# Weight sums moved from GpSimd to VectorE, kept in DRAM and reloaded; forms reloaded in place; one activation table for Ln and Exp

## The chip, the cores and the metric

One core of a Trainium2 chip runs the kernel. The metric is the device time in microseconds (us) of one execution. A core's engines work in parallel, each on its own queue of instructions in a fixed order: TensorE (PE, with its weight loads as PEld), VectorE (DVE), ScalarE (ACT), GpSimd (POOL) and SyncE (SP), which here issues all DMAs.

## The reference

One layer of a diffusion trunk, in float32, over 2048 latent tokens and 256 context tokens of 1024 channels:

```python
h = rmsnorm(x, norm_g) * (1 + scale) + shift          # hc likewise from ctx
v, g_b, g_c, z_a, u, z_b, m_a, m_b = split(h @ w_in)  # eight blocks of 1024
xc = grid_conv(u, conv4_w, 2) + conv4_b
y_lru = forward and backward RG-LRU scans of xc, started from the context's final states
y_a = g_b * grid_conv(g_c * v, conv3_w, 1) * silu(z_a)
y_b = y_lru * silu(z_b)
merged = sigmoid(m_a) * (y_a @ w_out_a) + sigmoid(m_b) * (y_b @ w_out_b)
x = rmsnorm(x + gate * (merged @ w_o), final_g)
```

shift, scale and gate come from a product of silu(c) with w_ada. An RG-LRU direction has two block-diagonal gates (128x128 blocks), a decay a = exp(-8 r softplus(-lambda)) and a linear recurrence over the tokens.

## The kernel before, in words

**Arithmetic.** Channels lie on the 128 partitions (8 blocks of channels, K = 8, H = 4), tokens along the free axis in four tiles of 512 (T), two tiles to a half. Each float32 matrix is split into a rounded part and a rest (`split2`, L426: ACT copies x to hi as fp32r, DVE subtracts lo = x - hi), and a product is three passes: hi hi, lo hi, hi lo (`passes`, L462).

**Pairs.** In the sweeps and in the second projection a product of two blocks of output channels with two token tiles is made with seven half products in place of eight (`class Pair`, L531; p1 to p7, each 12 matmuls of 512 columns). For that the tokens are combined into seven *forms* (B11, B21, B22, T1 to T4, four tiles each, with hi and lo 56 tiles), and the weights of two output blocks, r1 and r2, into parts A to D. Part A is r1 itself. `prep_d` (L547) makes the sums: s = r2's upper plus lower half (this is D), r2's upper half from r1 minus r2 (r2 is then C), and two more that turn r1 into B: four additions of 128x512 in a chain, all on POOL (`TT(..., eng="POOL")`, L274). `prep_a`, `prep_d`, `prep_bc` then split A, D, B, C.

**Order.** `sweep(half, c)` (L1030) treats channel block c of one half of the tokens with four pairs: L (LRU input and merge gate A), G (conv C gate and value), B (conv B gate and SiLU gate), Z (LRU SiLU gate and merge gate B). Between the pairs stand the gates' matmuls (bdp), convolutions, decays and scans. Eight first sweeps (half 0; block 0 starts with plain products, and only its Z is a pair) are followed by the projection of y_a (`merged_a`, L1181), eight second sweeps (half 1), `merged_a(1)`, `merged_b(1)` (L1192, four pairs ob10 to ob13), the output product `wo1`, `merged_b(0)` (pairs ob00 to ob03) and the last output product with the final norms (L1369 to L1408). In the first sweeps the context's 256 tokens of the same block run too: `ctx_gemm` (L708) multiplies raw r1 of the L pair, in float32, with the modulated context, four tiles hc that are kept in hc_dram and reloaded for each block from 1 on; three conv steps, gates and scans follow.

**Forms in DRAM.** T3, T4 and B22 go through fm_dram: `rest` (L1021) loads each into a T tile and then splits it with `put` into two F tiles. `gathered` (L1136) does the same with ya and with half of mg.

**Memory.** Tiles come from pools of numbered slots (SLOTS, L31): T 17 tiles of 128x512, F 64 of the same size in fp32r, W 6 of 128x1024 (split weights), D 2 of 128x512 (split D), R 3 of 128x1024 (raw weights), S 1 of 128x512 (s). A pool's buffers take their slots in the order in which the program first writes them.

**Planner.** Nothing is issued as written: every operation goes to `Plan` (L81) with an engine and a cost (`act_us`, `dve_us`, POOL 0.2 + 0.0027 a column, a DMA by its KB). `once` (L142) is a list scheduler: PE keeps the order of the program, and on ACT, DVE, POOL and SP the operation that can start first goes first, ties by how late it may be. A DMA that needs a slot is held back to 18 us ahead of PE (AHEAD). What it finds is each engine's fixed order on the chip, where an instruction waits for its semaphores, and all behind it on that engine too. TABLE (L36) gives Ln and Exp different tables, and a switch costs 1.3 in the plan.

**Norms.** `Stats` (L500) sums squares (ACT squares, DVE or, for x2, x3 and the context, POOL adds); `rs` sums over partitions with a product by ones (tile ss), and `rsq` (L480) makes the inverse root by Ln, Exp(-0.5 .) and three DVE steps.

Of the kernel before, what the change touches and what calls it, by code (L numbers as in the profile page):

```python
# [8 lines left out]
F32 = mybir.dt.float32  # L9
# [6 lines left out]
P = 128  # L16
D = 1024
# [18 lines left out]
TABLE = {AF.Sigmoid: "sigmoid", AF.Exp: "exp", AF.Tanh: "exp", AF.Sqrt: "sqrt", AF.Ln: "ln"}  # L36


class Buf:
# [214 lines left out]
def trunk(ctx: ExitStack, tc: tile.TileContext, par, sel2, xT, ctxT, wada, wgate, crow, win, woa, wob, wo, lru, out):  # L254
# [109 lines left out]
    pk_dram = dram("pk_dram", K, 2, 3, P, T)  # L364
    yb_dram = dram("yb_dram", 2, K, 2, P, T)
    mg_dram = dram("mg_dram", 2, K, 2, P, T)
    pa_dram = dram("pa_dram", 2, K, 2, P, T)
    z_dram = dram("z_dram", K, 2, P, T)
    kept = {}
# [60 lines left out]
    def put(name, x, bias=None):  # L430
# [6 lines left out]
            STT(lo.v, x, bias, hi.v, AD, SU)  # L437
        return hi, lo

    def fetch(name, src, kb=512, after=()):  # L440
        r = Buf("R", name)
        DMA(r.v, src, kb, after)
        return r

# [84 lines left out]


    class Pair:  # L531
        def __init__(self, name, s1, s2, after=()):
            self.name, self.s1, self.s2 = name, s1, s2
            self.r1 = fetch(name + "r1", s1, after=after)
            self.r2 = None
            self.after = after

        def second(self):
            if self.r2 is None:
                self.r2 = fetch(self.name + "r2", self.s2, after=self.after)  # L540

        def prep_a(self):
            n = self.name
            self.fa = Buf("W", n + "Ah"), Buf("W", n + "Al")
            split2(self.fa[0].v, self.fa[1].v, self.r1.v, 2 * T)

        def prep_d(self):  # L547
            n = self.name
            self.second()
            r1, r2 = self.r1, self.r2  # L550
            s = self.s = Buf("S", n + "s1")
            TT(s.v, r2[:, :H, :], r2[:, H:, :], AD, eng="POOL")
            TT(r2[:, :H, :], r1[:, :H, :], r2[:, :H, :], SU, eng="POOL")
            TT(r1[:, :H, :], s.v, r1[:, :H, :], SU, eng="POOL")
            TT(r1[:, H:, :], r1[:, H:, :], r1[:, :H, :], SU, eng="POOL")
            self.fd = Buf("D", n + "Dh"), Buf("D", n + "Dl")
            split2(self.fd[0].v, self.fd[1].v, s.v)

        def prep_bc(self):
            n = self.name  # L560
            self.fb = Buf("W", n + "Bh"), Buf("W", n + "Bl")
# [63 lines left out]
    class Lru:  # L625
# [79 lines left out]
            return i  # L705


        def ctx_gemm(self, raw, hcs=None):  # L708
# [10 lines left out]
            self.split("c", xc[:, :CTX], CTX)  # L719

        def ctx_gates(self, d):
            c = self.c
# [122 lines left out]
        return r  # L845

    def raw0(name, src):
        r = Buf("R", "r" + name)
        queue(DMA(r.v, src, 512))
        return r  # L850

    def matvec(m):

        row = ps(f"row{m}")
        for k0 in (0, H):
            mms = [(sc[:, k, :], wc[m, k].v, k0 == 0, k0 == H) for k in range(k0, k0 + H)]
            ins = [sc.v] + [x for _, x, _, _ in mms] + ([row.v] if k0 else [])

            def emit(mms=mms):
                for j, (w, x, a, z) in enumerate(mms):  # L860
# [3 lines left out]
        rows = Buf("S", f"rows{m}")  # L864
        rv = rows.m(lambda t: t.rearrange("p a b -> p (a b)"))
        A(rv, row.v, AF.Copy)
        return rv
# [147 lines left out]
        DMA(dbuf("fm_dram", 0, j), x21, 256)  # L1015
    raw = fetch("rawL", win[4 * K])
    lr.ctx_gemm(raw, hcs)
    a = unit("aZA1", wZA, bt1)
    cv.za(1, a.v)

    def rest(form, kinds, biased=True):  # L1021

        for n, i in kinds:
            for j in range(H):
                x = tb(n + "x")
                DMA(x.v, dbuf("fm_dram", i, j), 256)
                form[n].append(put(f"{n}_{j}", x.v, shf(H + j) if i == 2 and biased else None))


    def sweep(half, c, state, form):  # L1030

        plain_start = half == 0 and c == 0
        ss = srcs(c)
        n = f"{half}{c}"
        lr, cv = state["lr"], state["cv"]
        tail = state.pop("tail", [])
        pl = pg = None
        if plain_start:
            rest(form, (("T3", 1), ("T4", 0)))
            pz = Pair("Z" + n, *ss[3])  # L1040
            pz.p1(form)
            lr.ctx_gates(0)
        else:
            pl = state.pop("pl", None) or Pair("L" + n, *ss[0])
# [16 lines left out]
            pg = Pair("G" + n, *ss[1])  # L1061
# [11 lines left out]
            pb = Pair("B" + n, *ss[2])  # L1073
# [12 lines left out]
            lr.decay(1)  # L1086
            za1 = pb.p7(form)
            pz = Pair("Z" + n, *ss[3])
            pz.p1(form)
            cv.za(0, pb.p4(form).v)  # L1090
            lr.forward(1)
# [26 lines left out]
                lr.forward(1)  # L1118
            state["tail"][0] = late
        if c + 1 < K:  # L1120
            nl = state["lr"] = Lru(half, c + 1)
            state["cv"] = Conv(half, c + 1)
            nl.weights()
            if half == 0:
                state["pl"] = Pair(f"L{half}{c + 1}", *srcs(c + 1)[0])
                nl.ctx_gemm(state["pl"].r1)

    def stats(t):
        s = Stats(f"x{t}", eng="POOL")
# [4 lines left out]
        return s  # L1134

    def gathered(key, half, k, t, name):  # L1136
        x = tb(name)
        DMA(x.v, dbuf(key, half, k, t), 256)
        return put(name, x.v)
# [326 lines left out]
```

## Time and profile before

| | |
|---|---|
| runs, median (range) | 1947.99 us (1946.63 to 1950.41), 3 runs |
| profiled execution, own time | 1946.85 us |
| its span | 1945.1 us |
| PE busy | 1895.3 us, 97% |
| DVE busy | 1579.1 us, 81% |
| ACT busy | 1135.8 us, 58% |
| POOL busy | 507.3 us, 26% |
| DMA | 307.89 MB, 158 GB/s over the span |

The span runs from the first to the last instruction of the profiled execution; its own time is the device time of that execution. Busy times are unions of instructions on an engine; matmuls overlap each other, and their ends are modelled. L277 is the line of `TT`, so all additions of tiles stand under it, on POOL or DVE; L284 is `STT`, L271 ACT's `A`, L319 PE's `MM`, L327 the DMAs. Tiles carry the pair's name: G05r is the raw weight of pair G of half 0, block 5, Ah and Al its split part A, y, x, z its PSUM tiles, a and u what is copied out of them.

### The profile page before, as it was taken

The numbers are of one execution on the slowest core, as the hardware profiler recorded it, in microseconds if no ns is written. First come the engines' busy times: TensorE is split into PE (matmuls) and PEld (weight loads), VectorE is DVE, ScalarE is ACT, GpSimd is POOL, SyncE is SP. The second block draws the span as 40 slices with busy tenths as digits, with TensorE's granted clock in tenths as the row PEclk, the third lists the DMA queues.
The fourth block names the chain that finished last, engine by engine and source line by source line (L and its number), as shares of the span: only waits on it lengthen the run. The fifth ranks groups of instructions, "written<-read, shape, count | busy, mean of one in ns | idle before, by whom it ended". The sixth has DMA issues, their size and how long they took to land.

```text
span 1945.1 us, 24314 instructions
## 1 busy us (share of the span) xinstructions
PE 1895.3 (97%) x8546; PEld 1558.2 (80%) x8546; DVE 1579.1 (81%) x2050; ACT 1135.8 (58%) x1604; POOL 507.3 (26%) x305
## 2 busy tenths in 40 slices
PE   6999999999999999999999999999999999999997
PEld 3777888888888888888888888888888888788787
DVE  6897877878687878868898988989898778769854
ACT  6589676767677777346556575565756333435332
POOL 0222332332524230023233333242341022012100
PEclk9999999999999999999999999999999999999998
DMA  9152414233342416851442514324243985777933
GB/s 346 60 197 87 136 65 141 87 131 116 122 155 84 136 65 232 298 194 48 154 146 76 169 54 157 123 100 150 73 157 118 345 307 184 258 249 243 337 115 117
DMA packets 145419, 307.89 MB, mean 158 GB/s; under 512 B 16272, under 2 KB 20496, under 8 KB 145296
## 3 DMA queue, kind: packets, MB, share of 16 engines
q1 hardware_dynamic: 145296, 306.34, 45.9%
q8 instruction: 67, 1.10, 0.2%
q14 instruction: 56, 0.46, 0.1%
HBM read 218.19 MB, written 88.08 MB: 157 GB/s over the span
## 4 chain that ended last, share of the span: by engine, by line
PE 69%; DVE 13%; DMA 8%; ACT 6%; issue 4%; SPq 0%; POOL 0%; DVEq 0%; ACTq 0%; POOLq 0%
PE oa L319 9%; PE ao L319 4%; PE bdp L319 4%; PE wo L319 3%; ACT L271 2%; DVE xc L284 2%; DVE i L303 1%; DMA wc<-wada 1%; PE ac L319 1%; DMA pal<-pa_dram 1%; DMA pk<-pk_dram 1%; DMA x<-xT 1%; DMA mg<-mg_dram 1%; DMA sb<-smb_dram 1%; PE Z17y L319 1%
## 5 line engine op out<-in xcount | busy, mean ns | idle before, releaser
L271 ACT ACT_TABLE_LOAD x152 | 195.0, 1283 | 3.6 <-PEq L1457 0.7
L303 DVE TENSOR_TENSOR_SCAN i<-a,st,i 128x512 f32<-128x512 f32 x48 | 77.3, 1623 | 0.0
L277 DVE TENSOR_TENSOR i<-i,r 128x512 f32<-128x512 f32 x64 | 67.7, 1059 | 0.0
L284 DVE SCALAR_TENSOR_TENSOR r<-a,r 128x512 f32<-128x512 f32 x64 | 47.0, 755 | 16.9 <-ACT r L271 16.9
L271 ACT ACTIVATE xh<-xc 128x512 fp32r<-128x512 f32 x32 | 20.2, 632 | 58.0 <-DVE xc L284 58.0
L277 DVE TENSOR_TENSOR i<-i,xc 128x512 f32<-128x512 f32 x64 | 51.4, 822 | 0.4 <-ACT i L271 0.4
L271 ACT ACTIVATE a<-r,ns 128x512 f32<-128x512 f32 x64 | 46.0, 720 | 0.7 <-DVE i L277 0.2
L271 ACT ACTIVATE r<-bdp,pr 128x512 f32<-128x512 f32 x64 | 44.0, 687 | 1.3
L271 ACT ACTIVATE i<-bdp,pr 128x512 f32<-128x512 f32 x64 | 44.0, 687 | 0.0
L271 ACT ACTIVATE r<-r,hs 128x512 f32<-128x512 f32 x64 | 43.2, 712 | 0.0
L284 DVE SCALAR_TENSOR_TENSOR zz<-ao,gates,xr 128x256 f32<-128x256 f32 (+1 forms) x24 | 13.7, 572 | 35.1 <-PE ao L319 34.5
L271 ACT ACTIVATE sq<-zz 128x256 f32<-128x256 f32 (+1 forms) x21 | 10.3, 488 | 50.0 <-DVE zz L284 49.9
L271 ACT ACTIVATE r<-r 128x512 f32<-128x512 f32 x64 | 37.7, 624 | 0.4
L277 DVE TENSOR_TENSOR xl<-xc,xh 128x512 fp32r<-128x512 f32 x32 | 32.1, 1002 | 3.7 <-ACT xh L271 3.7
L277 DVE TENSOR_TENSOR sa<-oa,sa 128x512 f32<-128x512 f32 x32 | 21.7, 685 | 13.2 <-DMA sa<-sma_dram 7.0
L277 DVE TENSOR_TENSOR y<-y,sg 128x512 f32<-128x512 f32 x32 | 29.0, 907 | 0.0
L284 DVE SCALAR_TENSOR_TENSOR ri<-acc,ri 128x256 f32<-128x256 f32 x16 | 7.1, 452 | 26.3 <-ACT ri L271 26.3
L277 DVE TENSOR_TENSOR yx<-yx,yx 128x512 f32<-128x512 f32 x32 | 24.2, 758 | 4.5 <-DMA yx<-yb_dram 2.3
L277 POOL TENSOR_TENSOR ob00s<-ob00r 128x512 f32<-128x512 f32 x1 | 1.3, 1304 | 92.5 <-DMA fm_dram<-yx 92.5
L277 POOL TENSOR_TENSOR ob10s<-ob10r 128x512 f32<-128x512 f32 x1 | 1.3, 1287 | 88.4 <-DMA ob10r<-wob 88.4
L277 POOL TENSOR_TENSOR L10s<-L10r 128x512 f32<-128x512 f32 x1 | 1.3, 1294 | 87.5 <-DMA L10r<-win 87.5
L303 DVE TENSOR_TENSOR_SCAN pk<-pk,st,pk 128x512 f32<-128x512 f32 x16 | 20.4, 1277 | 4.5 <-DMA pk<-pk_dram 4.5
(15371 smaller groups left out, 7400.4 us busy)
## 6 DMA issues: line engine op xcount, KB each, us to landing
pk<-pk_dram SPq DMA_DIRECT2D x48, 256.0 KB, 5.6
wc<-wada SPq DMA_DIRECT2D x32, 256.0 KB, 6.0
ya_dram<-y SPq DMA_DIRECT2D x32, 256.0 KB, 3.3
pk_dram<-i SPq DMA_DIRECT2D x32, 256.0 KB, 2.2
roa<-woa SPq DMA_DIRECT2D x16, 512.0 KB, 4.5
ya<-ya_dram SPq DMA_DIRECT2D x32, 256.0 KB, 5.1
sa<-sma_dram SPq DMA_DIRECT2D x32, 256.0 KB, 5.0
pa_dram<-sa SPq DMA_DIRECT2D x32, 256.0 KB, 5.2
```

The source lines that it names most:

```text
L271: act.activation(o.ap(), i.ap(), func, **kw)
L277: return plan.add(Op(eng, d, lambda: e.tensor_tensor(o.ap(), a.ap(), b.ap(), op=op)), [o], [a, b])
L284: dve.scalar_tensor_tensor(o.ap(), a.ap(), s.ap() if isinstance(s, V) else s, b.ap(), op0=op0, op1=op1, **kw)
L303: dve.tensor_tensor_scan(o.ap(), a.ap(), u.ap(), init.ap() if isinstance(init, V) else init, op0=M, op1=AD)
L319: pe.matmul(o.ap(), w.ap(), x.ap(), start=a, stop=z, skip_group_check=True)
```

## The change

- **Sums on DVE.** `TT` sends every addition to DVE, whatever eng says: the four sums of each pair, the squares of x2, x3 and the context, and the four T1 differences of block 0.
- **Sums kept.** A pair of the first sweeps gets `at=(i, c)` and stores s, r1 (now B) and r2 (now C) to wd_dram, wb_dram and wc_dram after the sums: 28 pairs of blocks 1 to 7 and Z of block 0. The same 29 pairs of the second sweeps are made with `old=True`: they load A from the input and D, B, C from DRAM, each into a slot of the pool of its parts, and make no sums. L, G and B of block 0 in half 1, and the eight pairs of the projections, still make their sums (on DVE), without storing them.
- **Pools.** R and S are gone; W has 9 slots and D 3. Raw weights now take slots of W, s one of D, in one order with the split parts.
- **Forms in place.** `put_from` loads a form, ya or mg into the F tile that becomes its lo part, and splits there. No T tile is used.
- **Context of block 1.** Its L weight is fetched, and its `ctx_gemm` run, right behind that of block 0, with the context's tiles still on chip; the split follows later, where the product stood before.
- **One table.** In `rsq`, Ln and Exp are given the same table in the plan, and that set, natural_log_exp_and_others, is loaded by name ahead of the first of them.

```diff
-SLOTS = {"T": (17, (P, T), F32), "F": (64, (P, T), F32R), "W": (6, (P, K, P), F32R), "D": (2, (P, H, P), F32R),
-         "R": (3, (P, K, P), F32), "S": (1, (P, H, P), F32), "ps": (6, (P, T), F32), "bd": (2, (P, T), F32)}
+SLOTS = {"T": (17, (P, T), F32), "F": (64, (P, T), F32R), "W": (9, (P, K, P), F32R), "D": (3, (P, H, P), F32R),
+         "ps": (6, (P, T), F32), "bd": (2, (P, T), F32)}
...
     def TT(o, a, b, op, n=T, eng="DVE"):
-        e = {"DVE": dve, "POOL": pool}[eng]
+        eng = "DVE"; e = dve
...
+    def put_from(name, src, bias=None):
+        lo, hi = fb(name + "l"), fb(name + "h")
+        raw = lo.m(lambda t: t.bitcast(F32))
+        DMA(raw, src, 256)
+        if bias is None:
+            split2(hi.v, lo.v, raw)
+        else:
+            A(hi.v, raw, AF.Identity, bias=bias)
+            STT(lo.v, raw, bias, hi.v, AD, SU)
+        return hi, lo
...
     def rsq(r, ss, tmp, n=T):
-        A(r, ss, AF.Ln, bias=epsd.v, scale=1.0 / D, n=n)
-        A(r, r, AF.Exp, scale=-0.5, n=n)
+        for op in (A(r, ss, AF.Ln, bias=epsd.v, scale=1.0 / D, n=n), A(r, r, AF.Exp, scale=-0.5, n=n)):
+            op.table = LN_EXP
...
         def prep_d(self):
             n = self.name
-            self.second()
+            if self.old:
+                rd, self.rb, self.rc = (self.land(p, f, dbuf(f"w{f.lower()}_dram", *self.at), kb)
+                                             for p, f, kb in (("D", "D", 256), ("W", "B", 512), ("W", "C", 512)))
+                self.fd = self.part("D", "D", rd, T)
+                return
+            self.r2 = fetch(n + "r2", self.s2, after=self.after)
...
+            if self.at:
+                for t, r, kb in (("wd_dram", s, 256), ("wb_dram", r1, 512), ("wc_dram", r2, 512)):
+                    DMA(dbuf(t, *self.at), r.v, kb)
...
     lr.ctx_gemm(raw, hcs)
+    pl1, lr1 = Pair("L01", *srcs(1)[0], at=(0, 1)), Lru(0, 1)
+    lr1.ctx_gemm(pl1.r1, hcs, False)
...
-                x = tb(n + "x")
-                DMA(x.v, dbuf("fm_dram", i, j), 256)
-                form[n].append(put(f"{n}_{j}", x.v, shf(H + j) if i == 2 and biased else None))
+                form[n].append(put_from(f"{n}_{j}", dbuf("fm_dram", i, j), shf(H + j) if i == 2 and biased else None))
...
+        def pair(i, c=c):
+            return Pair("LGBZ"[i] + f"{half}{c}", *srcs(c)[i], at=(i, c) if c or i == 3 else None,
+                        old=half == 1 and (c > 0 or i == 3))
...
+    loaded = None
     for op in order:
+        if op.table and op.table != loaded:
+            loaded = op.table
+            if loaded == LN_EXP:
+                act.preload_act_table_set(LN_EXP)
```

## Rows read from the trace of the kernel before

**Rows 1.** The page, busy time of each engine, share of the span and instructions:
```profile
PE 1895.3 (97%) x8546; PEld 1558.2 (80%) x8546; DVE 1579.1 (81%) x2050; ACT 1135.8 (58%) x1604; POOL 507.3 (26%) x305
```

**Rows 2.** Windows by stage: length, busy PE, PEld, DVE, ACT, POOL, PEclk, DMA, GB/s:
```profile
60.00:180.00 120.00, 113.64 (x504) 92.43 (x503) 105.50 (x149) 92.13 (x141) 29.89 (x18) 1.00 0.39 130
180.00:759.00 579.00, 574.81 (x2559) 474.50 (x2558) 460.25 (x563) 411.92 (x576) 198.50 (x116) 1.00 0.35 117
...
850.00:1503.00 653.00, 650.05 (x2863) 536.69 (x2862) 588.55 (x702) 398.64 (x543) 213.46 (x122) 1.00 0.34 116
...
1592.00:1673.00 81.00, 79.25 (x350) 65.15 (x348) 68.19 (x82) 34.59 (x51) 16.95 (x10) 1.00 0.68 231
...
1800.00:1847.00 47.00, 42.70 (x183) 33.65 (x181) 39.04 (x51) 15.12 (x21) 6.26 (x4) 1.00 0.95 336
...
1932.00:1945.10 13.10, 1.44 (x7) 0.64 (x5) 5.01 (x12) 3.87 (x5) 0.00 (x0) 0.63 0.25 80
```

**Rows 3.** Waits of PE: waiter, what it waited for, us in total, times, longest:
```profile
PE bdp L319 <- ACT ri L271: 2.9, 1, 2.9
...
PE aL L319 <- ACT B_0h L271: 1.9, 1, 1.9
...
PE L05y L319 <- ACT L05u L271: 1.6, 1, 1.6
```

**Rows 4.** Timeline, 502 to 515 us: start, us, instruction, [idle before <- releaser]:
```profile
502.43 1.73 POOL L277 TENSOR_TENSOR G05s<-G05r 128x512 f32<-128x512 f32 x1
...
503.52 1.72 DVE L277 TENSOR_TENSOR G05Al<-G05r,G05Ah 128x1024 fp32r<-128x1024 f32 x1
...
505.16 1.76 DVE L284 SCALAR_TENSOR_TENSOR xc<-L05a,pr,xc 128x504 f32<-128x504 f32 x1
...
506.85 1.77 DVE L277 TENSOR_TENSOR Z04u<-Z04u,zs 128x512 f32<-128x512 f32 x1
508.16 1.62 POOL L277 TENSOR_TENSOR G05r<-G05r 128x512 f32<-128x512 f32 x1
508.55 1.77 DVE L284 SCALAR_TENSOR_TENSOR xc<-L05a,pr,xc 128x504 f32<-128x504 f32 x1
...
510.41 0.63 ACT L271 ACTIVATE xh<-xc 128x512 fp32r<-128x512 f32 x1 [4.87 <-DVE xc L284]
...
514.02 0.58 ACT L271 ACTIVATE L05u<-L05y 128x512 f32<-128x512 f32 x1
```

**Rows 5.** Groups of DVE, clear of POOL: instruction, count | busy, mean ns | idle:
```profile
L277 DVE TENSOR_TENSOR sa<-oa,sa 128x512 f32<-128x512 f32 x32 | 21.7, 685 | 13.2 <-DMA sa<-sma_dram 7.0 <-PE oa L319 6.2
...
L284 DVE SCALAR_TENSOR_TENSOR xc<-aL,pr,xc 128x504 f32<-128x504 f32 (+1 forms) x6 | 4.4, 735 | 7.5 <-ACT xc L271 7.4
```

**Rows 6.** Waits of SP's queue:
```profile
SPq L327 <- DVE Z15Bl L277: 19.0, 1, 19.0
```

**Rows 7.** Timeline of SP, 1100 to 1130 us:
```profile
1103.09 0.41 SPq L327 DMA_DIRECT2D B13r<-win  x1
```

**Rows 8.** Timeline of PE, 1113 to 1128 us:
```profile
1113.20 0.39 PE L319 MATMUL L13z<-B_0h,L13Bh 128*128 128x512 f32 x1
...
1126.80 0.39 PE L319 MATMUL B13y<-B_0h,B13Ah 128*128 128x512 f32 x1
```

**Rows 9.** Timeline of ACT, 108 to 134 us:
```profile
130.12 0.63 ACT L271 ACTIVATE T_3h<-T4x 128x512 fp32r<-128x512 f32 x1 [1.51 <-DMA T4x<-fm_dram]
```

**Rows 10.** Timeline of the end, 1933 to 1937 us:
```profile
1933.30 1.28 ACT L271 ACT_TABLE_LOAD   x1
...
1933.34 0.70 PE L319 MATMUL ss<-sq,ones 128*128 128x256 f32 x2 [0.59 <-ACT sq L271]
1934.60 0.47 ACT L271 ACTIVATE zz1256ss<-ss,epsd 128x256 f32<-128x256 f32 x1
1935.09 1.28 ACT L271 ACT_TABLE_LOAD   x1
```

**Rows 11.** DMA issues: tensors, count, KB each, median us from issue to landing:
```profile
roa<-woa SPq DMA_DIRECT2D x16, 512.0 KB, 4.5
```

More of the change, by code (lines that the diff above doesn't have):

```diff
@@ L36 @@
 TABLE = {AF.Sigmoid: "sigmoid", AF.Exp: "exp", AF.Tanh: "exp", AF.Sqrt: "sqrt", AF.Ln: "ln"}
+LN_EXP = "natural_log_exp_and_others"
 class Buf:
@@ L366, in trunk @@
     mg_dram = dram("mg_dram", 2, K, 2, P, T)
+    wb_dram = dram("wb_dram", H, K, P, K, P)
+    wc_dram = dram("wc_dram", H, K, P, K, P)
+    wd_dram = dram("wd_dram", H, K, P, H, P)
     pa_dram = dram("pa_dram", 2, K, 2, P, T)
@@ L438, in put @@
         return hi, lo
+    def put_from(name, src, bias=None):
[8 more added lines that the diff above has]
+        return hi, lo
     def fetch(name, src, kb=512, after=()):
-        r = Buf("R", name)
+        r = Buf("W", name, dt=F32)
         DMA(r.v, src, kb, after)
@@ L531, in trunk, with __init__, land, part @@
     class Pair:
-        def __init__(self, name, s1, s2, after=()):
+        def __init__(self, name, s1, s2, after=(), at=None, old=False):
             self.name, self.s1, self.s2 = name, s1, s2
-            self.r1 = fetch(name + "r1", s1, after=after)
+            self.after, self.at, self.old = after, at, old
             self.r2 = None
[L536 to L540, printed above, removed]
+            if old:
+                self.r1 = self.land("W", "A", s1, 512)
+            else:
+                self.r1 = fetch(name + "r1", s1, after=after)
+        def land(self, pool, f, src, kb):
+            raw = Buf(pool, self.name + f + "r", dt=F32)
+            DMA(raw.v, src, kb, self.after)
+            return raw
+        def part(self, pool, f, raw, n=2 * T):
+            hi, lo = Buf(pool, self.name + f + "h"), Buf(pool, self.name + f + "l")
+            split2(hi.v, lo.v, raw.v, n)
+            return hi, lo
         def prep_a(self):
             n = self.name
+            if self.old:
+                self.fa = self.part("W", "A", self.r1)
+                return
             self.fa = Buf("W", n + "Ah"), Buf("W", n + "Al")
@@ L548, in prep_d @@
             n = self.name
-            self.second()
+            if self.old:
+                rd, self.rb, self.rc = (self.land(p, f, dbuf(f"w{f.lower()}_dram", *self.at), kb)
+                                             for p, f, kb in (("D", "D", 256), ("W", "B", 512), ("W", "C", 512)))
+                self.fd = self.part("D", "D", rd, T)
+                return
+            self.r2 = fetch(n + "r2", self.s2, after=self.after)
             r1, r2 = self.r1, self.r2
-            s = self.s = Buf("S", n + "s1")
+            s = self.s = Buf("D", n + "s1", dt=F32)
             TT(s.v, r2[:, :H, :], r2[:, H:, :], AD, eng="POOL")
@@ L557, in prep_d @@
             split2(self.fd[0].v, self.fd[1].v, s.v)
+            if self.at:
+                for t, r, kb in (("wd_dram", s, 256), ("wb_dram", r1, 512), ("wc_dram", r2, 512)):
+                    DMA(dbuf(t, *self.at), r.v, kb)
         def prep_bc(self):
             n = self.name
+            if self.old:
+                self.fb = self.part("W", "B", self.rb)
+                self.fc = self.part("W", "C", self.rc)
+                return
             self.fb = Buf("W", n + "Bh"), Buf("W", n + "Bl")
@@ L705, in backward, with ctx_gemm @@
             return i
-        def ctx_gemm(self, raw, hcs=None):
+        def ctx_gemm(self, raw, hcs=None, split=True):
             if hcs is None:
@@ L718, in ctx_gemm, with ctx_split @@
             self.S["xc", "c"] = xc[:, :CTX]
-            self.split("c", xc[:, :CTX], CTX)
+            if split:
+                self.ctx_split()
+        def ctx_split(self):
+            self.split("c", self.S["xc", "c"], CTX)
         def ctx_gates(self, d):
@@ L847, in raw0 @@
     def raw0(name, src):
-        r = Buf("R", "r" + name)
+        r = Buf("W", "r" + name, dt=F32)
         queue(DMA(r.v, src, 512))
@@ L863, in matvec @@
             plan.add(Op("PE", 1.5, emit, lat=0.3), [row.v], ins)
-        rows = Buf("S", f"rows{m}")
+        rows = Buf("D", f"rows{m}", dt=F32)
         rv = rows.m(lambda t: t.rearrange("p a b -> p (a b)"))
@@ L1039, in sweep @@
             rest(form, (("T3", 1), ("T4", 0)))
-            pz = Pair("Z" + n, *ss[3])
+            pz = pair(3)
             pz.p1(form)
@@ L1043, in sweep @@
         else:
-            pl = state.pop("pl", None) or Pair("L" + n, *ss[0])
+            pl = state.pop("pl", None) or pair(0)
             pl.p1(form)
@@ L1060, in sweep @@
             merge_gate("sma_dram", half, c, 1, ma1.v, ma1.v)
-            pg = Pair("G" + n, *ss[1])
+            pg = pair(1)
             pg.p1(form)
@@ L1072, in sweep @@
             v1 = pg.p7(form)
-            pb = Pair("B" + n, *ss[2])
+            pb = pair(2)
             pb.p1(form)
@@ L1087, in sweep @@
             za1 = pb.p7(form)
-            pz = Pair("Z" + n, *ss[3])
+            pz = pair(3)
             pz.p1(form)
@@ L1120, in sweep @@
         if c + 1 < K:
-            nl = state["lr"] = Lru(half, c + 1)
+            early = plain_start
+            nl = state["lr"] = lr1 if early else Lru(half, c + 1)
             state["cv"] = Conv(half, c + 1)
@@ L1124, in sweep @@
             if half == 0:
-                state["pl"] = Pair(f"L{half}{c + 1}", *srcs(c + 1)[0])
-                nl.ctx_gemm(state["pl"].r1)
+                state["pl"] = pl1 if early else pair(0, c + 1)
+                if early:
+                    nl.ctx_split()
+                else:
+                    nl.ctx_gemm(state["pl"].r1)
     def stats(t):
@@ L1136, in gathered @@
     def gathered(key, half, k, t, name):
-        x = tb(name)
-        DMA(x.v, dbuf(key, half, k, t), 256)
-        return put(name, x.v)
+        return put_from(name, dbuf(key, half, k, t))
     def gather(key, half, name):
```

## The prediction

> **What bounds the kernel now.** I read the page first, then the windows by stage, the waits of PE, one stall in the timeline, and the end. The page shows PE busy for 1895.3 of 1945.1 us, POOL for 507.3 us [rows 1]. The change removes no matmul, so about 1895 us stay and only PE's idle time can be won. The windows say where that lies [rows 2], each stretch's length less PE's busy time: 6.4 us from 60 to 180 us, 4.2 in the first sweeps (180 to 759), 2.9 in the second (850 to 1503), 1.8 in the first paired projection (1592 to 1673), 4.3 in the second (1800 to 1847), and an end of 13.1 us with PE almost still. The opening's idle time hangs on its loads; I leave it alone.
>
> Next, why PE stands still in a sweep. One row of PE's waits is the 1.6 us for L05u on ACT [rows 3]. The timeline of that moment [rows 4] is the key: POOL makes the four sums of a pair (502.43 to 509.78), and beside it four DVE instructions with both inputs in SBUF take 1.72 to 1.77 us. Alone, such instructions of 512 columns take 0.685 and 0.735 [rows 5]. ACT's xh waits 4.87 us for the last of them, and the L05u that PE needs, in order behind xh, comes at 514.02. So POOL's sums, meant to be free, are paid on DVE, then on ACT, then on PE.
>
> **The parts, each with its cost.** The sum is made against the profiled execution's 1946.85 us, whose span is 1945.1; the runs' median is 1.1 above it, added at the end.
>
> *Sums from POOL to DVE.* A set of four costs DVE now, by [rows 4], 7.0 us for four instructions (1.72 + 1.76 + 1.77 + 1.77) worth about 3.5 alone (1.37, twice 0.685, for the 1,024 columns of G05Al, and 0.735 + 0.685 + 0.735): 3.5 lost. On DVE the set costs 4 x 0.685 = 2.7 [rows 5]. A first sweep (four sets) so wins 4 x 0.8 = 3 us of DVE, with DVE near 80% busy [rows 2]: about level. A second sweep makes no sums for its 29 reloaded pairs and wins 4 x 3.5 = 14 us of some 83. What is queued behind the moved sums on DVE are the splits and gate products of the same pair; four sums there are 2.7 us long against 7.35 on POOL, so the pair's parts come sooner, not later. Of the 4.2 us of the first sweeps I take 3.0 as won (bounds 0 and 4.2), since DVE still is 80% full and the planner's own costs for DVE, which know no POOL, then come true. Of the 2.9 in the second, 2.6; of the 1.8 in the first projection, whose eight pairs move their sums too, 1.3.
>
> *Sums kept and reloaded.* Adds 29 x 3 stores (1,280 KB a pair, 38 MB) and 29 x 768 KB more loads (23 MB). A first sweep moves 5.2 MB more in 87 us, 60 GB/s beside 117 at a DMA share of 0.35 [rows 2]: an estimate of 0.53. A second gets 38 GB/s beside 116: 0.45. Both are far from the 0.95 that the same window view shows at the end. So bandwidth costs nothing. What can cost is order. With R and W one ring of nine, I work out from the order of allocation that a pair's first load can't start before the former pair's second product is over. That is 1113.20 for B13, and the product that needs its weights begins at 1126.80: a lead of 13.6 us [rows 8]. Before, the load went out at 1103.09, a lead of 23.7 [rows 7]. Needed are 4.5 us for 512 KB [rows 11] and two splits of 1,024 columns, estimated at 1.4 each: 7.3. Cover 13.6 against need 7.3: zero, with 6.3 us in hand. The stores wait on SP for DVE, and loads are queued behind them; SP already waits up to 19.0 us for one split [rows 6], so this is the upper bound, kept for the rivals.
>
> *Forms in place.* Same loads and splits, but a load needs a slot of F rather than of T. T4's fourth load is late before: ACT's T_3h waits 1.51 us for it, ri behind it, and PE 2.9 us for ri [rows 9, 3]. I take that for a full T pool (17 slots). At the switches of stage F's slots come free three to eight products ahead, and by [rows 8] four products with two gate groups take 13.6 us: 8 us or more, which covers a load. At the end (1800 to 1847) the DMA engines are 0.95 busy [rows 2], and the bytes don't change: I take 0.8 of 4.3 (bounds -3 and +4.3).
>
> *Context of block 1.* Its 16 short matmuls (some 3.5 us) move from after that 2.9 us wait to before it, and fill it. Its four reloads go; its three conv passes come onto DVE earlier, and 15 sums in the stretch do too (some 9 us), against POOL's slowing of DVE there (29.9 us busy by [rows 2], half of it lost, 14). Of 6.4 us I take 3.5; bounds -3 (DVE, 88% busy there, gets worse) and 6.4.
>
> *One table.* In the opening the load saved I cost at nothing; the 1.9 us that PE waits for B_0h [rows 3] bounds it. At the end it is on the path [rows 10]: the load before Ln ends at 1934.58, the sums were ready at 1934.04, so 0.5 us goes; the load before Exp, 1.28, goes too. Sum 1.8, if the set stays loaded through Square; bounds 0 and 1.8. The Trainium skill (ScalarE: Activation LUTs, What ACT_TABLE_LOAD costs) gives some 1.38 us of drain beyond the 1.28 of each load. By it two loads would give back up to 4.6, an estimate, and the time would be 2.8 lower. The rows disagree: Ln starts 0.02 us after its load [rows 10].
>
> *Sum.* 3.0 + 2.6 + 1.3 + 0.8 + 3.5 + 1.8 = 13.0; 1946.85 - 13.0 = 1933.9, and with the 1.1 to the median 1935.
>
> **Rivals.** *A, DVE takes back what POOL gave.* The first sweeps, the opening stretch and the last projection win nothing, as DVE's 3 us a sweep are within what its order varies; left are 2.6 + 1.3 + 1.8 = 5.7, 1942.3. For it: DVE at 88% from 60 to 180 us. Against it: [rows 4]. *B, the ring and SP's order starve PE (slower).* A split behind a late load becomes PE's last wait. It decides once the lead falls below 7.3 us, that is once SP holds a load more than 6.3 us behind a store that waits for DVE, or a store's landing holds a slot. At 1 us for each of the 29 reloaded pairs it costs 29 against 13 won: 1964; at half that, 1949.5. For it: the 19.0 us of [rows 6] and a lead cut from 23.7 to 13.6. Against it: the sums are done before the former pair's units run, and SP had room. *C, the table part doesn't do what it says*, because another set is loaded between Ln and Square: 1.8 less, 1936.8. *D, a table load costs ACT more than its row shows*, by a stop after it. The gap after each load at the end is at most 0.02 us [rows 10], so what goes beyond the forecast is 0.04 in all, some 1935; with the page's drain for it the time would be 1932.2.
>
> **The numbers.** Forecast 0.60, A 0.16, B 0.20, C 0.03, D 0.01. About 0.2%, 3.9 us, is what a measurement of this kernel can tell from no change. Faster by more (below 1944.1): 0.60 + 0.04 of C and D + 0.06 of A, whose bounds straddle it = 0.70. Same: 0.07 of A and 0.03 of B = 0.10. Slower: 0.17 of B and 0.03 of A = 0.20. The range: all idle time of the five stretches gone and the bound of the opening won would be 1948 - 19.6 - 1.8 - 1.9 = 1924.7; I stop at 1927. Upwards it takes A and B to 0.6 us a reloaded pair, 1952.
>
> **What would show it.** Right: POOL nearly empty; DVE's xc, i and Cl at 0.7 and 1.2 us everywhere; DVE about 61 us in a second sweep (588.55 of 653 us now [rows 2], 75 of 83, less 14); PE's waits for u gone from the sweeps; no table load between Ln and Exp; the stretch 60 to 180 us with under 3 us idle. A would show the waits for u still there in the first sweeps. B would show PE waiting for Al or Ah, and behind those for DMA or a store, in the second. I am wrong in kind if PE's matmuls themselves change their pace, or if idle time appears in stages where there is none now.

## The result, and the profile after

The changed kernel takes 1928.67 us (median of 4 runs, 1927.54 to 1929.46); the kernel before, beside it, 1948.83 (1946.63 to 1950.41). The ratio is 0.9897, with a 95% interval of 0.988 to 0.9914: 20 us faster, inside the range forecast (1927 to 1952) but only 1.7 us above its lower end, and 6 us below the 1935 forecast. The profiled executions give the span that the sections below take apart: 1945.1 before, 1927.7 after, 17.4 less; the one before lies 2.0 us below its kernel's median, the one after 0.8 above.

The page of the kernel after, in its busy line (beside [rows 1]) and its DMA queue:

```profile
PE 1894.1 (98%) x8546; PEld 1563.1 (81%) x8546; DVE 1450.8 (75%) x2235; ACT 1129.3 (59%) x1597; POOL 0.2 (0%) x4
...
q1 hardware_dynamic: 165600, 366.11, 54.2%
```

POOL is empty, and DVE, which took over its additions, is 128 us less busy. PE's busy time is unchanged to 1.2 us. DMA moved 367.65 MB, 60 more.

The windows of both kernels, cut where the program passes the same point: opening up to pair L02, first sweeps, second sweeps, ob1 and ob0 (the two paired projections, `merged_b(1)` and `merged_b(0)`), last product, tail. The columns are those of [rows 2]. Before:

```profile
0.00:228.90 228.90, 204.10 (x909) 157.21 (x910) 189.01 (x303) 162.64 (x244) 53.79 (x38) 0.99 0.49 169
228.90:759.00 530.10, 525.91 (x2343) 434.00 (x2342) 415.06 (x506) 376.45 (x527) 181.90 (x108) 1.00 0.35 116
846.00:1503.30 657.30, 654.35 (x2882) 540.23 (x2881) 591.69 (x706) 400.50 (x545) 214.30 (x123) 1.00 0.35 117
1590.30:1668.50 78.20, 76.45 (x337) 63.01 (x336) 64.05 (x76) 33.22 (x48) 18.31 (x12) 1.00 0.67 227
1756.00:1837.50 81.50, 78.87 (x342) 63.61 (x341) 69.96 (x87) 32.59 (x46) 18.82 (x12) 1.00 0.79 271
1837.50:1934.05 96.55, 94.28 (x589) 84.02 (x587) 53.48 (x95) 32.80 (x55) 0.00 (x0) 1.00 0.43 146
1934.05:1945.10 11.05, 0.00 (x0) 0.00 (x0) 4.53 (x11) 2.71 (x4) 0.00 (x0) 0.56 0.29 95
```

After:

```profile
0.00:227.20 227.20, 207.87 (x910) 161.07 (x911) 180.28 (x337) 159.43 (x241) 0.20 (x4) 0.97 0.56 198
227.20:750.60 523.40, 523.40 (x2343) 434.60 (x2342) 403.66 (x618) 386.38 (x540) 0.00 (x0) 1.00 0.50 178
837.60:1491.40 653.80, 653.11 (x2882) 540.48 (x2881) 493.40 (x720) 409.26 (x558) 0.00 (x0) 1.00 0.46 158
1578.40:1656.50 78.10, 76.45 (x337) 63.01 (x336) 62.83 (x89) 34.23 (x52) 0.00 (x0) 1.00 0.74 255
1743.60:1822.50 78.90, 78.21 (x342) 63.74 (x341) 70.70 (x104) 34.14 (x50) 0.00 (x0) 1.00 0.86 304
1822.50:1918.50 96.00, 94.00 (x589) 83.92 (x587) 52.10 (x92) 24.99 (x47) 0.00 (x0) 1.00 0.41 143
1918.50:1927.70 9.20, 0.00 (x0) 0.00 (x0) 4.53 (x11) 0.89 (x2) 0.00 (x0) 0.56 0.35 114
```

Read length first: the first sweeps lost 6.7 us, the second 3.5, ob0 2.6, the tail 1.85, the opening 1.7, the last product 0.55, ob1 0.1. With 0.4 in wo1 that is the 17.4; the projections of y_a (oa, 87.0 each) did not move. In the first sweeps PE is now busy for all of the 523.40 us, while DVE does 112 instructions more in 11 us less.

The stall of [rows 4] shows why. The timeline of DVE after, in the same pair:

```profile
500.21 1.22 DVE L278 TENSOR_TENSOR G05Al<-G05r,G05Ah 128x1024 fp32r<-128x1024 f32 x1
501.41 0.69 DVE L278 TENSOR_TENSOR G05s<-G05r 128x512 f32<-128x512 f32 x1
502.02 0.74 DVE L285 SCALAR_TENSOR_TENSOR xc<-L05a,pr,xc 128x504 f32<-128x504 f32 x1
502.68 0.69 DVE L278 TENSOR_TENSOR G05r<-G05r,G05r 128x512 f32<-128x512 f32 x1
503.28 0.74 DVE L285 SCALAR_TENSOR_TENSOR xc<-L05a,pr,xc 128x504 f32<-128x504 f32 x1
503.93 0.69 DVE L278 TENSOR_TENSOR G05r<-G05s,G05r 128x512 f32<-128x512 f32 x1
504.53 0.69 DVE L278 TENSOR_TENSOR Z04u<-Z04u,zs 128x512 f32<-128x512 f32 x1
505.14 0.69 DVE L278 TENSOR_TENSOR G05r<-G05r 128x512 f32<-128x512 f32 x1
505.74 0.69 DVE L278 TENSOR_TENSOR xl<-xc,xh 128x512 fp32r<-128x512 f32 x1
```

These are the split, convolution steps and gate product that took 1.72 to 1.77 us each; they now take 1.22, 0.74 and 0.69, with the four sums among them. PE's wait for L05u is gone. The longest waits left to PE after its first 60 us, bdp's in the opening and the others behind it (columns of [rows 3]):

```profile
PE bdp L320 <- ACT r L272: 3.1, 1, 3.1
...
PE ob13y L320 <- ACT ob13u L272: 1.7, 1, 1.7
PE ao L320 <- DVE wo02l L278: 1.1, 1, 1.1
...
PE Z17y L320 <- ACT Z17u L272: 0.7, 1, 0.7
PE ob03y L320 <- ACT ob03u L272: 0.7, 1, 0.7
```

ACT's timeline at the end, beside [rows 10]: square, Ln, Exp, and no table load.

```profile
1917.32 0.42 ACT L272 ACTIVATE sq<-zz 128x256 f32<-128x256 f32 x1 [2.52 <-DVE zz L285]
1918.53 0.47 ACT L272 ACTIVATE zz1256ss<-ss,epsd 128x256 f32<-128x256 f32 x1 [0.79 <-PE ss L320]
1919.04 0.42 ACT L272 ACTIVATE zz1256ss<-zz1256ss 128x256 f32<-128x256 f32 x1
```

Five things were changed at once. The experiments ask which of them earned the 20 us, and whether POOL's slowing of DVE, or the lateness of the sums themselves, was what PE had waited for. The second question is answered only in part.

### The profile page after: what moved, and what is told of

The parts are those of the page before. It is cut to its first block, busy times and chain, and to the rows that moved or that the text cites. A ratio compares the mean times of both kernels' runs of the same rounds, so it can differ in the third digit from the quotient of the medians.

```text
span 1927.7 us, 24094 instructions
## 1 busy us (share of the span) xinstructions
PE 1894.1 (98%) x8546; PEld 1563.1 (81%) x8546; DVE 1450.8 (75%) x2235; ACT 1129.3 (59%) x1597; POOL 0.2 (0%) x4
## 2 busy tenths in 40 slices
DMA packets 165721, 367.65 MB, mean 191 GB/s; under 512 B 18528, under 2 KB 22752, under 8 KB 165600
## 4 chain that ended last, share of the span: by engine, by line
PE 95%; DMA 2%; DVE 1%; ACT 1%; SPq 0%; issue 0%; DVEq 0%; ACTq 0%
PE oa L320 9%; PE bdp L320 5%; PE wo L320 5%; PE ao L320 4%; PE ac L320 1%; DMA wc<-wada 1%; PE bdc L320 1%; PE ob03y L320 1%; PE Z17y L320 1%; PE Z07y L320 1%; PE L07y L320 1%; PE ob00y L320 1%; PE L03y L320 1%; PE L05y L320 1%; PE L04y L320 1%; PE L02y L320 1%
## 5 line engine op out<-in xcount | busy, mean ns | idle before, releaser
L304 DVE TENSOR_TENSOR_SCAN i<-a,st,i 128x512 f32<-128x512 f32 x48 | 60.5, 1275 | 0.0
L278 DVE TENSOR_TENSOR i<-i,xc 128x512 f32<-128x512 f32 x64 | 42.8, 688 | 13.7 <-ACT i L272 13.0
L278 DVE TENSOR_TENSOR i<-i,r 128x512 f32<-128x512 f32 x64 | 43.1, 684 | 0.0
L285 DVE SCALAR_TENSOR_TENSOR zz<-ao,gates,xr 128x256 f32<-128x256 f32 (+1 forms) x24 | 13.6, 572 | 30.5 <-PE ao L320 29.0
L278 DVE TENSOR_TENSOR sa<-oa,sa 128x512 f32<-128x512 f32 x32 | 21.8, 687 | 17.4 <-PE oa L320 9.6
L278 DVE TENSOR_TENSOR xl<-xc,xh 128x512 fp32r<-128x512 f32 x32 | 22.1, 691 | 13.1 <-ACT xh L272 13.1
L272 ACT ACTIVATE sq<-z 128x512 f32<-128x512 f32 x14 | 8.9, 633 | 25.3 <-DVE z L285 22.8
L304 DVE TENSOR_TENSOR_SCAN pk<-pk,st,pk 128x512 f32<-128x512 f32 x16 | 20.5, 1281 | 2.6 <-DMA pk<-pk_dram 2.6
L278 DVE TENSOR_TENSOR y<-y,sg 128x512 f32<-128x512 f32 x32 | 21.9, 684 | 0.0
L285 DVE SCALAR_TENSOR_TENSOR z<-wo,gates,xr 128x512 f32<-128x512 f32 x16 | 12.0, 749 | 12.1 <-PE wo L320 11.9
L285 DVE SCALAR_TENSOR_TENSOR xcc<-ac,pr,xcc 128x255 f32<-128x255 f32 (+1 forms) x24 | 11.5, 480 | 6.1 <-ACT xcc L272 5.9
L272 ACT ACTIVATE T_0h<-T_0l 128x512 fp32r<-128x512 f32 x8 | 5.0, 624 | 16.5 <-DMA T_0l<-fm_dram 16.5
```

Of the source, the lines that this page charges most:

```text
L272: act.activation(o.ap(), i.ap(), func, **kw)
L285: dve.scalar_tensor_tensor(o.ap(), a.ap(), s.ap() if isinstance(s, V) else s, b.ap(), op0=op0, op1=op1, **kw)
L304: dve.tensor_tensor_scan(o.ap(), a.ap(), u.ap(), init.ap() if isinstance(init, V) else init, op0=M, op1=AD)
```

## The experiments

Each variant is planned anew, so every engine's order may differ in places that its edit doesn't touch. Ratios are to the kernel before, on the same chip. Idle time of PE is the length of a stretch less PE's busy time in it.

**One part at a time.** The sums alone, on the kernel before: both halves make them on DVE, nothing is stored, and tables, forms and context stay as they were.

```diff
     def TT(o, a, b, op, n=T, eng="DVE"):
-        e = {"DVE": dve, "POOL": pool}[eng]
+        eng = "DVE"; e = dve
```

> The kernel before with one part of the change: every addition on DVE, none on POOL. Sums are made in both halves, nothing is kept. Theory (POOL slows DVE, DVE delays ACT, ACT delays PE): instructions of DVE with two inputs in SBUF fall back to 0.68 to 0.75 us, PE's idle time in the first sweeps falls from 4.2 us to under 1 and in the second from 2.9 to under 1, and the time falls by 6 to 12 us. Rival (the gain is the reload's and the new pools', and the sums only change engine): idle time in the sweeps stays within 2 us of before, and the time within 3 us. Second rival: with 16 sums a sweep on DVE in the second sweeps too, DVE has 72 us of work in 83 and the time rises.

Measured 0.9895 (0.9879 to 0.9912), 1928.93 us: the whole gain, from one line, and more than the 6 to 12 us expected. The windows of its first and second sweeps:

```profile
227.80:751.20 523.40, 523.40 (x2343) 434.73 (x2342) 397.18 (x614) 374.88 (x525) 0.00 (x0) 1.00 0.35 117
...
838.20:1492.00 653.80, 653.11 (x2882) 540.57 (x2881) 553.01 (x828) 400.27 (x544) 0.00 (x0) 1.00 0.35 117
```

To the 0.1 us these are the lengths after. With all its sums on DVE a second sweep's DVE is still 39 us less busy than before over the eight (591.69), and has 100 us to spare.

The table alone, in the kernel before (`op.table = LN_EXP` for Ln and Exp, and the load by name):

> The kernel before with Ln and Exp in one table and nothing else. Theory by the prediction's term: 1.8 us less at the end and nothing in the opening, so 1.8 less in all. Rival (the opening's 3.3 us came from the table too, since the plan knows of the shorter norm and puts ACT's B_0h ahead of V00h): PE's 1.9 us wait for B_0h goes, the opening's idle time falls from 18.4 to about 15, and the time falls by about 5.

Measured 0.9992 (0.9979 to 1.0005), 1948.26. The tail is 9.23 us, 1.8 shorter as worked out, and PE's 1.9 us wait for B_0h is gone; but the opening up to L02 takes 232.1 us in place of 228.9, with PE at a granted clock of 0.50 from 36.6 to 40.0 and from 77.6 to 84.4, where it had only one such stretch before (20.5 to 23.9). That execution, the fastest of the ten (1944.56), is 2.4 us shorter than the one before, because the sweeps, ob1 and ob0 are some 4 us shorter in it, which the edit doesn't touch. So the 1.8 at the end is won; what the other stretches give and take with a new plan is larger, and the total of the ten can't be told from no change.

The forms in place alone (`gathered` likewise):

```diff
-                x = tb(n + "x")
-                DMA(x.v, dbuf("fm_dram", i, j), 256)
-                form[n].append(put(f"{n}_{j}", x.v, ...))
+                form[n].append(put_from(f"{n}_{j}", dbuf("fm_dram", i, j), ...))
```

> The kernel before with forms, ya and mg loaded into the F tile that is split in place, and nothing else. Theory by the prediction's terms: the 2.9 us wait for ri near 131 us goes or shrinks, as T4's last load no longer waits for a T tile, and the rest stays: 2 to 3 us less. Rival (the load was late for the store before it, not for a T tile): that wait stays within 0.5 us, and the time too.

Measured 0.9992 (0.998 to 1.0003), 1949.01. PE's wait that I had put down to a full T pool is still there:

```profile
PE bdp L319 <- ACT ri L271: 3.1, 1, 3.1
```

But it has another form. ACT now splits T4's fourth tile (T_3h, at 132.98) without waiting for its load, and only behind the ri that PE wants (131.54). That ri stands behind the splits of T3 and T4, whose loads SP issues from 118.96 on, where T3's went out from 101.80 before. So taking no T tile didn't remove the wait; whether a T slot had held the load in the kernel before isn't shown.

**Everything but the sums.** The kernel after, with the additions back on POOL wherever the program says POOL; the reload stays, so half 1 makes hardly any.

```diff
-        eng = "DVE"; e = dve
+        e = {"DVE": dve, "POOL": pool}[eng]
```

> The kernel after with additions on POOL where the program says POOL: the first sweeps' sums, those of the eight pairs of the projections and of three pairs of the second half's block 0, and the norms' additions. Everything else of the change stays. Theory: the first sweeps get back their waits for u, 3 to 5 us, the second sweeps, which reload, stay free of them; the time is 4 to 7 us above the kernel after. Rival (the contention doesn't matter once T has room and weights are kept): within 2 us of the kernel after.

Measured 1.0003 (0.999 to 1.0016), 1950.7: reload, forms, context and table together bring nothing, and by the ratios this is some 20 us above the kernel after, not the 4 to 7 expected. Windows of the sweeps:

```profile
232.20:763.50 531.30, 526.11 (x2343) 434.00 (x2342) 408.73 (x510) 384.82 (x540) 171.02 (x107) 1.00 0.49 175
...
850.50:1504.30 653.80, 653.11 (x2881) 540.54 (x2880) 496.75 (x712) 406.87 (x558) 13.62 (x8) 1.00 0.46 158
```

The first sweeps have their idle time back (5.2 us). The second are as short as after: the reload does take the sums off POOL there. Of the 21.2 us by which the span (1948.9) is above that after, the first sweeps cost 7.9, the opening 5.0, and what follows the second sweeps 8.3, where PE idles 4.5 us in the last product. The reload cures the second sweeps, and so does DVE; one cure is enough, as the next run shows from the other side.

**No reload.** The kernel after, its second sweeps making their sums on DVE, and no stores:

```diff
-    pl1, lr1 = Pair("L01", *srcs(1)[0], at=(0, 1)), Lru(0, 1)
+    pl1, lr1 = Pair("L01", *srcs(1)[0], at=None), Lru(0, 1)
...
-            return Pair("LGBZ"[i] + f"{half}{c}", *srcs(c)[i], at=(i, c) if c or i == 3 else None,
-                        old=half == 1 and (c > 0 or i == 3))
+            return Pair("LGBZ"[i] + f"{half}{c}", *srcs(c)[i], at=None, old=False)
```

> The kernel after, but the second sweeps make their sums again on DVE, and nothing is stored or reloaded; pools, forms, context and table stay as after. Theory (the reload is worth nothing, since DVE has room for 16 sums in a second sweep): within 2 us of the kernel after, 1927 to 1931, PE's idle time in the second sweeps still under 1 us. Rival (the second sweeps are free of waits because the sums are gone from them): 1.5 to 3 us of waits for u come back there, 1931 or more.

Measured 0.9895 (0.9878 to 0.9911), 1926.24, with second sweeps of 653.78 us. Sixty megabytes of traffic buy nothing here, and cost nothing that can be told.

**The first half only.** On the kernel before, the sums of half 0, the norms' additions and the T1 differences move to DVE; the sums of half 1 and of the projections stay on POOL.

```diff
+            eng = "POOL" if n[1] == "1" or n.startswith("ob") else "DVE"
...
```

> The kernel before with all additions of the first half and of the norms on DVE, and the sums of the second half's pairs and of both paired projections left on POOL. Theory (each stretch pays for its own POOL work): the first sweeps' idle time goes (4.2 to under 0.5) and the opening's falls by 3 to 4, the second sweeps and the paired projections keep their 2.9, 1.8 and 2.6; the time is 7 to 10 below the kernel before. Rival (the gain is the second half's, where DVE was 90% busy): less than 5 below.

Measured 0.9957 (0.9942 to 0.9973), 1939.15, 8 us less than the kernel before on that chip (1947.19). First sweeps 523.4 us, idle 0.0; second sweeps 658.08, idle 3.5; ob0 idle 2.8. Each of these stretches follows the place of its own sums. The opening doesn't show it: it takes 231.2 us (before 228.9) in the profiled execution, which was the slowest of the eight (1945.49).

**POOL kept busy for nobody.** Two runs put the sums on DVE and then load POOL with work that nobody waits for, to part POOL's slowing of DVE from the lateness of the sums. The first gives POOL eight products of 240 columns a pair:

```diff
+            for i in range(8):
+                TT(idle.v, idle.v, idle.v if i else al, M, 240, eng="idle")
```

> The sums are on DVE as in the run with the sums alone, and POOL makes, for each pair, eight multiplications of 240 columns of a tile of zeros that nobody waits for; the first reads one split part of the weights, so that they start with the pair. The output is unchanged. Theory (POOL's reading beside DVE is what costs): DVE's two-input instructions rise to 1.2 us and more again, idle time of 3 us and more comes back in the first sweeps, and the time is 10 us or more above the run with the sums alone. Rival (the sums were merely late on POOL, 7.4 us a chain in place of 2.7): nothing comes back, within 3 us of that run.

Measured 0.9938 (0.9923 to 0.9953), 1934.78: by the ratio 12 of the 20 us are left, a smaller loss than the 10 us expected. POOL is busy for 538.1 us and DVE for 1674.8 (1510.0 with the sums alone), 0.31 us of DVE for each of POOL. PE's idle time in the sweeps stays as in the sums alone (0.0 and 0.69), with 177 us of POOL in the first sweeps; of the 6.1 us that its span (1933.2) is above the 1927.1 of the sums alone, 1.6 are in the opening (229.4 us) and 4.0 in the last product (98.07). The slowing did not reach that of POOL's own sums: the xc steps of the sweeps take 0.97 us on average (1.33 before, 0.74 alone), and the splits of 1,024 columns are not slowed at all. So the second run has four a pair, as wide as the sums:

```diff
+            for i in range(4):
+                TT(idle.v, four, four if i else al, M, T, eng="idle")
```

Here `four` is the tile of ones, spread to 128x512, and `al` the first half of the pair's Al; the result goes to a tile that is never read.

> As the run with the idle POOL, but with four multiplications of 512 columns a pair, the size of the sums, in place of eight of 240: in that run DVE's xc rose only to 0.97 us on average (1.33 in the kernel before) and the splits of 1,024 columns not at all, so the dose was too small. Theory (the slowing of DVE by POOL's reading is the cause): xc back at 1.2 us or more, some 3 us of waits for u back in the first sweeps, 7 us and more above the run with the sums alone, at 1936 or more. Rival (the waits came from the sums being late on POOL, so that ACT, in order, stood before the split of D): xc slow again, and still under 1 us of waits in either sweep.

Measured 1.0021 (1.001 to 1.0032), 1953.09: the whole gain is gone, and no wait of the trace is for POOL. The busy line of its page:

```profile
PE 1900.6 (97%) x8546; PEld 1559.5 (80%) x8546; DVE 1711.3 (88%) x2351; ACT 1132.7 (58%) x1603; POOL 433.9 (22%) x280
```

Its group of DVE's scans (total and mean of 48; the mean is 1275 ns after, 1623 before):

```profile
L304 DVE TENSOR_TENSOR_SCAN i<-a,st,i 128x512 f32<-128x512 f32 x48 | 80.6, 1693 | 0.0
```

The windows of its sweeps:

```profile
232.30:757.50 525.20, 524.71 (x2343) 434.14 (x2342) 464.75 (x617) 373.42 (x526) 133.20 (x92) 1.00 0.34 117
...
844.50:1510.50 666.00, 658.96 (x2882) 538.91 (x2881) 651.07 (x832) 401.37 (x548) 206.62 (x124) 1.00 0.34 117
```

In the second sweeps 206.62 us of POOL add 98.1 us to DVE (651.07 less the 553.01 of the sums alone). The kernel before paid about as much: 214.30 us of POOL for 104 us of DVE (591.69 less the 493.40 after, in which eight sums take 5.5). But here DVE makes the sums as well: it is 98% busy, 90% before, PE stands idle for 7 us, and the stretch is 12.2 longer. PE's waits are not the same ones either: they are for G10u and for the L12a to L17a, before for L13u to L16u. So the run shows that work on POOL which nobody reads can cost as much as the whole change won; it doesn't show that the waits before came about in this way.

In the first sweeps it speaks against it. There POOL's 133.20 us add 67.6 us to DVE; at 464.75 us DVE is busier than before (415.06) or in e4 (408.73), and the xc steps take 1.17 us on average (1.38 before, 1.19 in e4). Yet only 0.5 us of idle time returns, not the 3 expected, where e4, with the sums themselves on POOL, has 5.2. Two differences are left between the idle work and the sums. On POOL the sums come late. And they slow the splits: a split of 1,024 columns takes 1.44 us on average in the first sweeps before (at most 2.33), but 1.22 in e9, where none runs beside POOL's work. The kernel before shows a chain of the first kind, in half 1, in its timelines of POOL, ACT and PE:

```profile
1185.68 2.02 POOL L277 TENSOR_TENSOR G14s<-G14r 128x512 f32<-128x512 f32 x1 [17.22 <-DMA G14r<-win]
...
1187.73 0.63 ACT L271 ACTIVATE G14Dh<-G14s 128x512 fp32r<-128x512 f32 x1 [5.68 <-POOL G14s L277]
...
1189.67 0.58 ACT L271 ACTIVATE L14u<-L14y 128x512 f32<-128x512 f32 x1
...
1190.30 0.50 PE L319 MATMUL L14y<-T_0h,L14Ch 128*128 128x512 f32 x1 [0.78 <-ACT L14u L271]
```

ACT stands 5.68 us before the copy of a sum, and the L14u that PE wants is behind it. How the 4.2 us of the first sweeps divide between late sums, slowed splits and the slowing of the rest of DVE stays open.

**The context back.** The kernel after, with block 1's context where it stood before, reloaded like the others (`early = False`, and the two lines in the opening removed):

> The kernel after with the context of block 1 where it was before, behind Z of block 0 and reloaded. Theory (moving it made the new 3.15 us wait of bdp at 142 us, with PE at the lower clock behind it): that wait goes, and the time is 3 to 5 below the kernel after. Rival (the wait belongs to the plan of all the other parts): within 1.5 us of the kernel after.

Measured 0.9896 (0.9881 to 0.9911), 1927.41. The 3.1 us wait of bdp goes, but one of 1.04 us (bdp for ri) and one of 1.88 us for the reloaded hc come, and PE's clock is 0.50 from 37.0 to 43.8. The early context moves a stall, and its total is that of the kernel after.

**The best two parts.** Sums on DVE and one table, on the kernel before:

> The kernel before with all additions on DVE and with Ln and Exp in one table, nothing else of the change. Theory (sums on DVE are worth all of the 20 us, the table 1.8 at the end, kept sums, forms and context nothing): 1927, that is 1.8 below the run with the sums alone, with an end of 9.2 us in place of 11.0. Rival (keeping the sums pays once the sums are on DVE, and the change needs its parts together): 1929 or more, above the kernel after.

Measured 0.9868 (0.9854 to 0.9883), 1921.79: 7 us below the sums alone and 7 below the kernel after, 5 to 6 by the ratios (the chips differ), and 5 below the 1927 expected. Tail 9.18; opening up to L02:

```profile
0.00:222.30 222.30, 205.19 (x911) 158.93 (x911) 179.60 (x337) 160.44 (x242) 0.20 (x4) 0.98 0.51 176
```

That is 4.9 us less than after. PE idles 2.2 us less there, and its clock falls less.

And these two with the forms in place:

> The kernel before with sums on DVE, one table and forms in place. Theory (forms in place are worth nothing where T is not what is waited for): within 1.5 us of the run with sums and table. Rival (they cost, since ya, mg and the forms then wait for slots of F): 2 us and more above it, with the 2 us of idle time in the last product that the kernel after has.

Measured 0.9865 (0.985 to 0.988), 1921.72: the same. The forms in place are worth nothing on top either.

Last, a try to mend ob13, where ACT stands before copies of mg whose loads land late. The planner's cost of a DMA's flight, 1.7 us beyond the wire, is raised in the version of two parts:

```diff
-                op.end = wire + 1.7
+                op.end = wire + 3.0
```

> The best so far (sums on DVE, one table) with a plan that reckons 3.0 us in place of 1.7 from a DMA's transfer to its use, nearer to what the DMA rows show. Theory (ACT stands before copies of mg whose loads land later than planned, with the u that PE needs behind them): the 0.9 us wait for ob13u goes and the time falls by 1 to 2. Rival (the plan's order is a matter of luck at this size): within 2 us to either side, with waits elsewhere.

Measured 0.9909 (0.9892 to 0.9925), 1929.37. The wait of ob13u falls from 0.9 to 0.7 us, and new ones come: 1.0 in oa, 3.5 for a copy of mg in the last product, 1.5 more in the opening, which is no longer for it (222.2 us). One constant in the plan is worth 8 us in places that it was not meant for. So a part that nets under some 8 us can't be judged by its total alone, and I judge the small ones by their stretch. Of the 7 us that the best two parts have over the sums alone, the 1.8 at the end are the table's; the rest, in the opening, may be the plan's.

## Why the prediction was right

The direction and the range held: 1928.67 against 1935 (1927 to 1952), near the lower end. The cause, the sums' place, is shown: with the sums alone the gain is there (e1), with all but them it is not (e4), and with one half's it comes in that half (e8). The path that the prediction gave, from POOL over DVE and ACT to PE, is shown in its first step (e7, e9); beyond the one stall read in [rows 4], no run shows that PE's waits in the first sweeps came from DVE's slowing and not from late sums. The size is partly luck: the terms add up to 13.0, the profiled spans differ by 17.4 and the medians by 20, and the terms missed to both sides. By its steps:

- *Sums to DVE, per set.* Right. DVE in a second sweep was forecast at about 61 us; it is 493.40 / 8 = 61.7, a win of 12.3 where 14 was forecast from a somewhat higher start. A first sweep was to save DVE 3.0 us; with the sums alone the six of that window (blocks 2 to 7) save 415.06 - 397.18 = 17.9, or 3.0 each.
- *First sweeps, 3.0 taken, 4.2 as bound: mis-sized.* They lost 6.7. All 4.2 us of idle time went, and 2.5 us of PE's busy time with them. A wait costs more than its idle row: after the 0.56 us wait at 537.26 in the kernel before, the first matmul takes 0.50 in place of 0.39 and the next starts 0.34 later in place of 0.23. From the last matmul before a wait to the first of the next product, each of the eight stops there (six of 0.2 to 1.6 us, two of 0.1) costs 0.29 to 0.30 beyond its idle time, 2.4 in all. The bound had counted only what stands as idle. The second sweeps (2.6 taken, 3.5 measured) have the same surplus. The doubt whether DVE has room fell with rival A: it has, once POOL is quiet.
- *Reload.* The costs were right: B13's first load is issued at 1104.36, its A is split at 1111.31, and its product begins at 1117.77. That is a lead of 13.4 us against a need of 7.0 (13.6 and 7.3 forecast). Rival B's waits for split weights don't appear. But the 14 us of DVE that I credited to it were not needed, as e6 shows.
- *60 to 180 us, 3.5: too large, and the reasons fell.* Idle time there fell from 6.4 to 4.2 us, not under the 3 us named as a sign. Loads without a T tile left PE's wait as long (e3), and the context moved the stall from one wait of bdp to another (e10). In the whole opening PE's idle time fell by 5.5 us (24.8 to 19.3), but half of PE's clock, from 38.8 to 42.2 and from 141.2 to 148.0, took much of that back, so the opening won 1.7.
- *First paired projection, 1.3: missed.* It won 0.1. With the sums alone it won 1.0 (77.2 us), as the wait for ob13u fell from 1.8 to 0.7. But that wait is 0.7 with the forms alone and 1.0 with the table alone too, and 1.7 after: it goes with the order of the plan, not with the sums' place alone. After, ACT stands in order before copies of mg whose loads have just landed:

```profile
1647.92 0.63 ACT L272 ACTIVATE mg_01h<-mg_01l 128x512 fp32r<-128x512 f32 x1 [0.25 <-DMA mg_01l<-mg_dram]
1649.10 0.63 ACT L272 ACTIVATE mg_05h<-mg_05l 128x512 fp32r<-128x512 f32 x1 [0.55 <-DMA mg_05l<-mg_dram]
1649.79 0.63 ACT L272 ACTIVATE mg_02h<-mg_02l 128x512 fp32r<-128x512 f32 x1
1650.33 0.58 ACT L272 ACTIVATE ob13u<-ob13y 128x512 f32<-128x512 f32 x1
```

- *Second paired projection and what follows, 0.8: too small.* ob0, wo1 and the last product won 3.6; I had credited it to the forms in place, but for ob0's 2.6 it is the sums of the four pairs: with these alone ob0 is 78.9 us, with the forms alone 83.9.
- *Table, 1.8 at the end: right* (1.85; alone 1.8). Rivals C and D fall: the set stays loaded through Square, and Ln followed its load by 0.02 us before. The 1.38 us of drain that the Trainium skill (ScalarE: Activation LUTs, What ACT_TABLE_LOAD costs) adds to a load would have made the tail 4.6 shorter; the trace does not show it. The opening's wait of 1.9 for B_0h, which was only a bound, went too, and other waits took its place.

What I did not see is that three of the five parts (reload, forms, context) bring nothing that can be told here, and the table no more for sure than its 1.8 us at the end: the sums' place is the change.

## What to carry to other kernels

Before work is moved to an engine that looks free, compare the busy engine's same instruction beside that work and away from it: here a POOL addition that seemed free (1.74 us on average in the second sweeps) cost DVE nearly half its own length, more than the 0.69 that the sum costs on DVE itself. Price a stall by the start of the next product, not by the idle row alone, and try each part of a bundle by itself: here the sums and the table without the rest were faster than all five parts. When a planner makes the order, know how far a harmless edit moves the total (8 us here) before a small gain is believed.

## What the hardware showed that was not expected

**POOL's work slows DVE's instructions with two inputs in SBUF, though neither waits for the other's data.** In e9 nobody reads POOL's tile, and DVE's scan still goes from 1275 to 1693 ns on average, with 0.47 us of DVE for each of POOL's in the second sweeps (98.1 / 206.62). The Trainium skill (SBUF — State Buffer, Who interferes with whom) says that such an instruction contends with a GpSimd instruction that reads SBUF, and calls the ports that the two share an exclusive lock. The trace agrees in kind: the xc steps, which take 0.735 us alone, take 1.76 and 1.77 beside sums of 1.61 to 2.15 [rows 4, 5]. The narrower work of e7 costs 0.31 us of DVE for each of POOL.

**The same wait of PE is followed by half its clock in one kernel and not in another.** The kernel after and e6 both have a wait of bdp of 3.15 us at the same place of the program. The windows from 137 us, after:

```profile
137.00:141.20 4.20, 1.84 (x9) 1.19 (x7) 4.20 (x10) 3.85 (x6) 0.00 (x0) 1.00 0.21 83
141.20:148.00 6.80, 6.01 (x14) 4.75 (x15) 3.54 (x5) 5.53 (x9) 0.00 (x0) 0.50 0.51 171
148.00:154.00 6.00, 6.00 (x27) 4.91 (x27) 2.74 (x4) 5.57 (x8) 0.00 (x0) 1.00 0.44 131
```

Without the reload (e6):

```profile
137.00:141.20 4.20, 1.05 (x6) 0.55 (x5) 4.20 (x9) 3.84 (x6) 0.00 (x0) 1.00 0.17 62
141.20:148.00 6.80, 6.80 (x31) 5.60 (x32) 3.31 (x5) 6.75 (x11) 0.00 (x0) 1.00 0.56 185
```

After, PE makes 14 matmuls in 6.01 busy us at 1.2 GHz (a granted clock of 0.50), and in e6 31 in 6.80 at 2.4; e6's opening is 3.7 us shorter (223.5 against 227.2), with PE idle about as long in it (19.0 and 19.3); it also lacks the half clock that the kernel after has from 21.7 to 25.1. What decides it was not tried.
